# Issuing the first output stores two batches earlier in a batched transposed matmul

## The chip, the cores and the metric

The kernel runs on one core of a Trainium2 chip. The metric is the device time of one execution in microseconds (us). The time before is the median of three runs: 124.31 us, between 124.25 and 124.97. One of these three, the one of 124.97 us, was recorded by the hardware profiler, and every line of a profile below comes from that execution.

## The reference

Sixteen independent products of 512 x 512 matrices in float32, with both operands transposed:

```python
batch, m, k, n = 16, 512, 512, 512
a: (batch, k, m)    b: (batch, n, k)
np.matmul(a.transpose(0, 2, 1), b.transpose(0, 2, 1)).astype(np.float32)
```

Each operand and the output hold 16 matrices of 1 MiB. A core has to read 33.55 MB and to write 16.78 MB.

## The kernel before

The sixteen batches are taken as eight pairs. Each engine has its own program; they meet at semaphores only, and inside one engine the order is the written order.

**Loads (SP).** SP issues all loads, on one DMA queue (q1 in the profile). One load brings both matrices of b of a pair (2 MiB, L122). For the pairs 1 to 5 one load brings both matrices of a (2 MiB, L103); for the pairs 0, 6 and 7 each matrix of a is a load of its own (1 MiB, L105). In the 2 MiB loads each partition reads 16 KB in one piece; in the 1 MiB loads 8 KB. There are three buffers for pairs of a, three for pairs of b and five for pairs of output (`OUTS = 5`). Where a load would bring data into a buffer in use, SP waits first: L101 for the matmuls of three pairs ago, L121 for the transposes of three pairs ago. From batch 10 on SP also waits at L125 until the store of five pairs ago has landed; this wait is put in SP's program ahead of the load of a, so that nothing of the pair can be copied into an output buffer which is still being stored. All later loads stand behind this wait in SP's order. So the load of the pair 5 of a waits for the store of pair 0, the load of batch 12 for the store of pair 1, and the load of batch 14 for the store of pair 2.

**Compute.** ACT casts each matrix of a to bf16 (L165 for the wide loads, in two instructions; L167 for the others). DVE casts b to bf16, half a pair at a time (L190). PE transposes b by matmuls with an identity (L243, the function `turn`), DVE copies the transposed b from PSUM to SBUF (L199), and PE multiplies (L257, the function `half`, 8 matmuls for one half of a batch). For every batch DVE copies the first half of the product from PSUM to the output buffer, and ACT the second (both L177). PE's loop over the pairs is: both halves of the even batch, the first transposes of the next pair, the first half of the odd batch, the second transposes, the second half of the odd batch.

**Stores.** The pairs 0 to 4 are stored by ACT, each by one DMA of 2 MiB on ACT's own queue (q10), issued in ACT's program right behind a copy-out (L225, which calls the function at L87; the profile has the issue at L90). A packet of a store holds 8 KB. The pairs 5, 6 and 7 are stored by SP on q1, behind all loads (L131 for 5 and 6, L135 and L137 for the two halves of 7). ACT's program is, for each batch i: cast batch i + 1, copy out batch i, and then, for some i, one store. Which one, `LAG` says (L223):

```python
j, odd = divmod(i - LAG, 2)
if odd and 0 <= j < H - TAIL:
    store(act, j)
```

With `LAG = 3` the pair j (batches 2j and 2j + 1) is stored behind the copy-out of batch 2j + 4.

**Semaphores.** There are twenty. Some serve two waits: `turned` also counts the last copies-out (as `last_go`), `id_go` also tells that ACT has drained (as `half_go`).

Of the kernel before, what the change touches and what calls it, by code (L numbers as in the profile page):

```python
# [11 lines left out]
def kernel(  # L12
# [29 lines left out]
    LOADS = 3  # L42
    PAIRS = 3
    OUTS = 5
    LAG = 3
    TAIL = 3
    H = B // 2
    STORED = H - (H - OUTS) + 1

    stored = tc.alloc_semaphore("stored")  # L50
# [3 lines left out]
    with tc.tile_critical(sync_engine=nc.gpsimd.engine):  # L54
        sb = lambda name, shape, dt: ctx.enter_context(nc.sbuf_tensor(name, shape, dt))
        ps = lambda name, shape, dt: ctx.enter_context(nc.psum_tensor(name, shape, dt))
        sem = tc.alloc_semaphore
# [10 lines left out]
        o_ps = [ps(f"o_ps{s}", [P, MO // 2, N], f32) for s in range(2)]  # L68


        a_in = [sem(f"a_in{s}") for s in range(2 * LOADS - 1)]
        b_in = [sem(f"b_in{s}") for s in range(PAIRS)]
        o_out = [sem(f"o_out{s}") for s in range(H - OUTS)]


        turned = last_go = sem("turned")
        summed = sem("summed")

        id_go = half_go = sem("id_go")

        bc_go = sem("bc_go")
        bt_go = sem("bt_go")
# [4 lines left out]
        def store(eng, j, part=slice(0, 2)):  # L87


            eng.dma_start(  # L90
                out_v[2 * j + part.start:2 * j + part.stop].rearrange("b p mo n -> p b mo n"),
                o_sb[j % OUTS][:, part],
            ).then_inc(o_out[j] if j + OUTS < H else stored, 16)

        def load_a(sp, i):

            q, g = divmod(i, 2)
            s, use = q % LOADS, q // LOADS
            if use:

                sp.wait_ge(summed, MO * (2 * (q - LOADS) + 1) + 1)  # L101
            if q in WIDE:
                sp.dma_start(a_sb[s][:], a_w[q]).then_inc(a_in[2 * s], 16)  # L103
            else:
                sp.dma_start(a_sb[s][:, g * KO:(g + 1) * KO], a_v[i]).then_inc(a_in[2 * s + g], 16)  # L105
# [7 lines left out]
        def run_sp(sp):  # L113
            for i in range(B):
                if i == 0:
                    load_a(sp, 0)


                for p in ([0] if i == 0 else [(i + 1) // 2] if i % 2 and i + 1 < B else []):
                    if p >= PAIRS:  # L120
                        sp.wait_ge(turned, p - PAIRS + 1)  # L121
                    sp.dma_start(b_sb[p % PAIRS][:], b_v[p]).then_inc(b_in[p % PAIRS], 16)  # L122
                if i % 2 == 0 and i // 2 >= OUTS:

                    sp.wait_ge(o_out[i // 2 - OUTS], 16)  # L125
                if i and not (i % 2 and i // 2 in WIDE):
                    load_a(sp, i)

            for j in range(H - TAIL, H - 1):
                sp.wait_ge(summed, MO * (2 * j + 2) + 3)  # L130
                store(sp, j)  # L131

            sp.wait_ge(summed, MO * (B - 1) + 1)
            sp.wait_ge(half_go, 3)
            store(sp, H - 1, slice(0, 1))  # L135
            sp.wait_ge(last_go, H + 1 + 3)
            store(sp, H - 1, slice(1, 2))  # L137

        def run_pool(pool):
# [30 lines left out]
        def copy_out(eng, i, rm, go):  # L170

            q = rm if isinstance(rm, int) else rm.stop - 1
            eng.wait_ge(summed, MO * i + q + 1)
            copy = eng.copy if eng is nc.scalar else eng.tensor_copy
            h = q // 2
            p = rm - 2 * h if isinstance(rm, int) else slice(None)
            copy(o_sb[i // 2 % OUTS][:, i % 2, rm, :], o_ps[h][:, p, :]).then_inc(go, 1)  # L177
# [40 lines left out]
        def run_act(act):  # L218
            cast_a(act, 0)
            for i in range(B - 1):  # L220
                cast_a(act, i + 1)
                copy_out(act, i, slice(2, 4), oa_go)
                j, odd = divmod(i - LAG, 2)  # L223
                if odd and 0 <= j < H - TAIL:
# [5 lines left out]
        def run_pe(pe):  # L230
# [41 lines left out]
            with pe.Fori(0, H) as _i:  # L272
# [6 lines left out]
                half(1, 1)  # L279

        run_sp(nc.sync)
        run_pool(nc.gpsimd)
        run_dve(nc.vector)
# [35 lines left out]
```

## Time and profile before

| what | value |
|---|---|
| time of the profiled execution | 124.97 us |
| its span, first to last instruction | 122.6 us |
| median of the three runs | 124.31 us |
| bytes read / written | 33.55 MB / 16.78 MB |
| mean DMA rate over the span | 411 GB/s |
| busy share PE / ACT / DVE | 70% / 55% / 46% |
| store issues on ACT's queue (pairs 0 to 4) | 42.34, 52.88, 63.98, 82.19, 96.28 us |
| last three store issues on SP's queue | 108.64, 112.52, 116.81 us |

Busy time counts compute instructions; DMA issues are not in it. "ACTq" and "SPq" mark an instruction of an engine's sequencer, here the issue of a DMA. The time to landing of a DMA is counted from its issue to the semaphore that tells its end; several transfers that wait in one queue have overlapping times. The 16 DMA engines of the core serve both queues, q1 and q10.

### The profile page before, as it was taken

How to read it: one execution, taken by the hardware profiler on the slowest of the kernel's cores; microseconds unless marked ns; L12 is line 12 of the kernel's file. 1: busy time of each engine (PE TensorE's matmuls, PEld its weight loads, DVE VectorE, ACT ScalarE, POOL GpSimd, SP SyncE). 2: the span in 40 equal slices, each digit the busy share in tenths (PEclk: the TensorE clock that was granted, in tenths of full speed). 3: DMA queues.
4: the chain of work that ended last, by engine and by line, in shares of the span. 5: the costliest groups of instructions: out<-in, count | busy, mean ns of one | idle time of the engine just before them, and what ended most of it. 6: DMA issues, size and time to landing. Idle time of an engine off the chain costs nothing. (4 is left out here: it accounts for less than half of the span.)

```text
span 122.6 us, 1085 instructions
## 1 busy us (share of the span) xinstructions
PE 85.2 (70%) x392; PEld 49.6 (40%) x400; DVE 56.2 (46%) x48; ACT 66.8 (55%) x44; POOL 0.7 (1%) x6
## 2 busy tenths in 40 slices
PE   0000949799799899979781992985996389979800
PEld 0000913564464365546331660324642237427500
DVE  0005276476937739574239160087549205270300
ACT  4150015778997997987994029976130590470210
POOL 2000000000000000000000000000000000000000
PEclk9999999999999999999998599589999955999997
DMA  3999999999999999999999999999999999999992
GB/s 64 449 428 428 414 446 428 428 428 428 428 428 428 428 412 409 414 417 436 433 417 441 454 417 414 430 428 452 414 422 428 428 428 425 428 428 428 425 428 118
DMA packets 4928, 50.33 MB, mean 411 GB/s; under 512 B 448, under 2 KB 448, under 8 KB 448
## 3 DMA queue, kind: packets, MB, share of 16 engines
q1 hardware_dynamic: 3568, 39.85, 77.1%
q10 hardware_dynamic: 1360, 10.49, 20.2%
HBM read 33.55 MB, written 16.78 MB: 411 GB/s over the span
## 5 line engine op out<-in xcount | busy, mean ns | idle before, releaser
L257 PE MATMUL o_ps<-bt_sb,a_bf 128*128 128x512 bf16 x248 | 64.1, 407 | 8.3 <-PEq L232 7.3
L257 PEld LDWEIGHTS o_ps<-bt_sb,a_bf 128*128 128x128 bf16 x256 | 29.2, 117 | 38.2 <-issue 16.2
L165 ACT CAST a_bf<-a_sb 64x2048 bf16<-64x2048 f32 x20 | 38.0, 1898 | 9.0 <-DMA a_sb<-in_a_dram 8.7
L243 PE MATMUL bt_ps<-identity,b_bf 128*128 128x128 f32 x144 | 23.6, 317 | 22.6 <-PEq L232 22.6
L177 DVE COPY o_sb<-o_ps 128x1024 f32<-128x1024 f32 x16 | 19.6, 1223 | 32.1 <-PE o_ps L257 32.1
L243 PEld LDWEIGHTS bt_ps<-identity,b_bf 128*128 128x128 f32 x144 | 21.6, 211 | 27.8 <-issue 26.8
L190 DVE CAST b_bf<-b_sb 128x2048 bf16<-128x2048 f32 x16 | 19.4, 1220 | 23.2 <-DMA b_sb<-in_b_dram 23.2
L177 ACT COPY o_sb<-o_ps 128x1024 f32<-128x1024 f32 (+1 forms) x17 | 16.4, 963 | 19.5 <-PE o_ps L257 19.4
L167 ACT CAST a_bf<-a_sb 128x2048 bf16<-128x2048 f32 x6 | 11.4, 1901 | 20.5 <-DMA a_sb<-in_a_dram 20.5
L199 DVE COPY bt_sb<-bt_ps 128x1024 f32<-128x1024 f32 x16 | 19.4, 1215 | 3.2 <-PE bt_ps L243 3.2
L167 ACT ACT_TABLE_LOAD x1 | 1.3, 1283 | 0.9 <-PEq L303 0.9
L144 POOL TENSOR_SCALAR_AFFINE_SELECT identity<-identity 128x128 f32<-128x128 f32 x1 | 0.3, 292 | 0.2 <-POOL identity L142 0.2
L142 POOL MEMSET identity<- 128x128 f32 x1 | 0.2, 204 | 0.7 <-POOLq L54 0.7
L303 POOL MEMSET const-bfloat16-1.0<- 128x1 bf16 x1 | 0.1, 101 | 0.0
L303 POOL MEMSET const-uint8-127<- 128x1 uint8 x1 | 0.1, 101 | 0.0
L303 POOL MEMSET const-float32-0.0<- 128x1 f32 x1 | 0.1, 98 | 0.2 <-issue 0.2
L303 POOL MEMSET const-float32-1.0<- 128x1 f32 x1 | 0.1, 98 | 0.0
## 6 DMA issues: line engine op xcount, KB each, us to landing
b_sb<-in_b_dram SPq DMA_DIRECT2D x8, 2048.0 KB, 20.5
a_sb<-in_a_dram SPq DMA_DIRECT2D x5, 2048.0 KB, 19.9
out_dram<-o_sb ACTq DMA_DIRECT2D x5, 2048.0 KB, 18.6
a_sb<-in_a_dram SPq DMA_DIRECT2D x6, 1024.0 KB, 15.6
out_dram<-o_sb SPq DMA_DIRECT2D x2, 2048.0 KB, 12.7
out_dram<-o_sb SPq DMA_DIRECT2D x2, 1024.0 KB, 5.7
```

Source lines behind the costliest of these rows:

```text
L142: pool.memset(identity[:], 0.0).then_inc(id_go, 1)
L144: pool.affine_select(out=identity[:], in_=identity[:], compare_op=mybir.AluOpType.not_equal, fill=1.0, base=0, pattern=[[-1, P]], channel_ ...
L165: copy = act.copy(to[s * P // 2:(s + 1) * P // 2], x[own, s * KO:(s + 1) * KO, :])
L167: copy = act.copy(to[:], x[:, g * KO:(g + 1) * KO, :])
L177: copy(o_sb[i // 2 % OUTS][:, i % 2, rm, :], o_ps[h][:, p, :]).then_inc(go, 1)
L190: dve.tensor_copy(to, x).then_inc(bc_go, n)
L199: dve.tensor_copy(bt_sb[g][:].rearrange("p j (ni r) -> p j ni r", r=NR), bt_ps[:].rearrange("p j r (g ni) -> p g j ni r", g=2)[:, g],).the ...
L243: last = pe.transpose(bt_ps[:, j, r, :], w[:, r, j, :], identity[:])
L257: last = pe.matmul(o_ps[h][:, q, :], a_r[:, rk, 2 * h + q, :], bt_h[:, rk // 2, rk % 2, :], start=(rk == 0), stop=(rk == KO - 1),)
L303: nc = _bacc.Bacc("TRN2", target_bir_lowering=False, num_devices=1)
```

## The change

Three things are edited.

`LAG` becomes 1, so that the pair j is stored behind the copy-out of batch 2j + 2: behind batch 2 for pair 0, 4 for pair 1, 6, 8 and 10 for the pairs 2, 3 and 4.

Semaphores are no longer shared: `last_go` and `half_go` get semaphores of their own, with constants for their own counts, and `a_in` has one more, which makes three.

`o_out`, which had one semaphore for each of the three stores that a load waits for, becomes one for each of the five output buffers; the waits at L125 are for the same three stores as before. With its two more there are twenty-five semaphores in all.

```diff
-    LAG = 3
+    LAG = 1
...
-        a_in = [sem(f"a_in{s}") for s in range(2 * LOADS - 1)]
+        a_in = [sem(f"a_in{s}") for s in range(2 * LOADS)]
         b_in = [sem(f"b_in{s}") for s in range(PAIRS)]
-        o_out = [sem(f"o_out{s}") for s in range(H - OUTS)]
-        turned = last_go = sem("turned")
+        o_out = [sem(f"o_out{s}") for s in range(OUTS)]
+        turned = sem("turned")
         summed = sem("summed")
-        id_go = half_go = sem("id_go")
+        last_go = sem("last_go")
+        half_go = sem("half_go")
+        id_go = sem("id_go")
...
-            ).then_inc(o_out[j] if j + OUTS < H else stored, 16)
+            ).then_inc(o_out[j % OUTS] if j + OUTS < H else stored, 16)
...
-                    sp.wait_ge(o_out[i // 2 - OUTS], 16)
+                    sp.wait_ge(o_out[i // 2 % OUTS], 16 * (i // 2 // OUTS))
...
-            sp.wait_ge(half_go, 3)
+            sp.wait_ge(half_go, 1)
             store(sp, H - 1, slice(0, 1))
-            sp.wait_ge(last_go, H + 1 + 3)
+            sp.wait_ge(last_go, 3)
             store(sp, H - 1, slice(1, 2))
```

## The prediction

> **What bounds the kernel now.** I read first the page's slices: the busy share of the DMA engines, and what they moved.
>
> ```profile
> PEclk9999999999999999999998599589999955999997
> DMA  3999999999999999999999999999999999999992
> GB/s 64 449 428 428 414 446 428 428 428 428 428 428 428 428 412 409 414 417 436 433 417 441 454 417 414 430 428 452 414 422 428 428 428 425 428 428 428 425 428 118
> ```
>
> From the second slice to the last but one the DMA engines are full, at some 428 GB/s. The bytes are the same after the change, so the sum of the traffic can't get shorter; only its order can change, and with it how much traffic is left when the compute ends. So I look at the end: the last copy-out and the last store's issue in the timeline, and that store's row among the DMA issues.
>
> ```profile
> 116.20 0.58 ACT L177 COPY o_sb<-o_ps 128x512 f32<-128x512 f32 x1 [0.32 <-PE o_ps L257]
> 116.81 0.34 SPq L90 DMA_DIRECT2D out_dram<-o_sb  x1
> out_dram<-o_sb SPq DMA_DIRECT2D x1, 1024.0 KB, 4.7
> ```
>
> The last store lands 4.7 us after its issue, at 121.5, and the span ends 1.1 later. The very first load, 1 MiB into an idle machine, took 4.9. So the last store hardly waits for others: both bounds meet here, and a compute end that comes later moves the end one for one.
>
> What sets the compute end? Going back from it, PE works with small gaps to 98.47. There it had stood still, and so had ACT:
>
> ```profile
> 96.27 1.90 ACT L167 CAST a_bf<-a_sb 128x2048 bf16<-128x2048 f32 x1 [5.37 <-DMA a_sb<-in_a_dram]
> 98.47 3.58 PE L257 MATMUL o_ps<-bt_sb,a_bf 128*128 128x512 bf16 x8 [2.41 <-PEq L232]
> ```
>
> ACT waited 5.37 us for a matrix of a, that of batch 13 (issued at 72.42, its row says 23.8 us to landing: 96.2). PE begins batch 13 when it is cast. So the chain is: batch 13 lands at 96.2, 20.6 us of compute follow up to the last issue at 116.81, then 4.7 and 1.1. The question of the change is when batch 13 lands, and that is set by how many bytes of stores get ahead of it.
>
> **How loads and stores share.** The DMA queues in a window in which both are at work, 46 to 62 us (packets, MB, share):
>
> ```profile
> DMA packets 607, 6.81 MB, mean 425 GB/s; under 512 B 48, under 2 KB 48, under 8 KB 48
> q1 hardware_dynamic: 304, 4.46, 65.1%
> q10 hardware_dynamic: 303, 2.35, 34.7%
> ```
>
> One packet of each in turn. A packet of a wide load is 16 KB and of a store 8 KB, so a store takes a third of the rate while it lasts; against a 1 MiB load (8 KB packets) it takes half. From 35.4 us (chosen below) to 96.2, the landing of batch 13, the two queues moved:
>
> ```profile
> DMA packets 2437, 25.86 MB, mean 425 GB/s; under 512 B 208, under 2 KB 208, under 8 KB 208
> q1 hardware_dynamic: 1365, 17.47, 68.0%
> q10 hardware_dynamic: 1072, 8.39, 32.6%
> ```
>
> 8.39 MB are exactly the stores of pairs 0 to 3.
>
> **Step 1, the issue times.** Now the store of pair 0 is issued just ahead of the copy-out of batch 4:
>
> ```profile
> 32.80 1.01 ACT L177 COPY o_sb<-o_ps 128x1024 f32<-128x1024 f32 x1
> ...
> 42.34 0.42 ACTq L90 DMA_DIRECT2D out_dram<-o_sb  x1
> 43.35 1.01 ACT L177 COPY o_sb<-o_ps 128x1024 f32<-128x1024 f32 x1
> ```
>
> The issue runs 1.0 us ahead of the copy's start, since the sequencer goes on while the cast still runs. The same spot behind batch 2 is 32.80 - 1.0 = 31.8. Its first packets came at 46.0, 3.7 after the issue (window by window: none of q10 at 45 to 46, 15 packets at 46 to 47), so now at 31.8 + 3.7 = **35.4**. Each later store j takes the place in ACT's program that j - 1 had: about 42.3, 52.9, 64 and 82 before delays. Each costs ACT's sequencer 0.38 us beside running casts, as now: nothing on a path; without that cover it would be 5 x 0.38, as it is today. One issue stands in each place as before, except that one place is added (batch 2) and one falls away (batch 12).
>
> **Step 2, is ACT's queue ever empty?** At a third of 425, 2.10 MB take 14.8 to 15.1 us; four stores keep q10 at work from 35.4 to about 80.7 for three, 95.8 for four. The fourth must be issued by 77, the fifth by 92, to follow without a hole. Even with their batches 4 us late (step 3) these issues are at 69 and 86. So q10 has work all the time.
>
> **Step 3, the loads.** The 17.47 MB of q1 hold two 1 MiB loads (batches 12 and 13), 2.10 MB, and 15.37 MB of wide packets. Beside them go 15.37 / 2 + 2.10 = 9.79 MB of stores, in place of 8.39. Together 27.26 MB at 425 GB/s are 64.1 us: batch 13 lands at 35.4 + 64.1 = **99.5, 3.3 us later**. The way there, counted back with 7.4 us for a wide load and 4.9 for a narrow one: b of pair 7 at 94.6 (now 91.0), batch 12 at 87.2 (84.3), b of pair 6 at 82.2 (80.2), a of pair 5 at 74.8 (72.7), b of pair 5 at 67.4 (63.2), a of pair 4 at 60.0 (56.0). All later, the first ones by 4.
>
> **Step 4, SP's gates.** This is what speaks for the change. SP waits today for stores before it may load:
>
> ```profile
> SPq L105 <- DMA out_dram<-o_sb: 20.0, 2, 10.7
> SPq L103 <- DMA out_dram<-o_sb: 15.7, 1, 15.7
> ```
>
> The 15.7 end at 61.06, when store 0 lands; q1 then runs dry, and from 62.5 to 64.5 the trace has 0.87 MB of stores and nothing of loads. With store 0 landing near 52 the load of pair 5 is issued some 9 us sooner and q1 is never empty. But a sooner issue only places it behind 2 wide loads that are now late themselves; the sum of step 3 already has q1 full throughout. The next gates (stores 1 and 2, about 67 and 82) open while 15 us of loads are queued. What q1 wins at 62 to 65 is some two thirds of 2 us; what it loses is a third of 10.6 us, 35.4 to 46.0, and the 84 to 86 us gap in q10, now filled.
>
> **Step 5, the end.** From batch 13's cast on nothing in the program changes: +3.3 to the last issue (120.1) and to the span (125.9). Batches 14 and 15 land near 103.6 and 106.1 (the fifth store's rest, then loads alone); their casts are due by 109 and 110. By 99.5 all but 8.9 MB are moved, some 21 us of traffic, so the DMA engines have holes of some 3 us between 110 and 123. No transfer is late next: compute is.
>
> **Step 6, the semaphores.** No wait is added; each waits for the event it waited for before, so neither a gain nor a new stall is there. Five more may have to be cleared: if the 1.1 us behind the last landing and the 2.4 us outside the span were all due to the twenty, five cost 0.9; the row nearest to it has no semaphore work at all, so I take 0 and keep 0 to 0.9.
>
> The sum against the profiled execution: 124.97 + 3.3 = 128.3. That execution lies 0.66 over the median; on the median it is 124.31 + 3.3 = **127.6**.
>
> **Bounds of the unknown.** The stores ahead of batch 13 are at least today's 8.39 MB (0 us) and at most all five, 10.49 MB: 27.96 / 0.425 = 65.8, +5.0. The clock: after gaps of 2.41 and 3.16 us (98.47, 67.10) PE ran at 0.50 for some 4 to 5 us, after one of 1.91 (84.06) it did not. At 98.47 that costs 3.58 against 1.99 for 8 matmuls and 1.91 against 1.20 for the transposes, 2.3 us. By my schedule PE again stands 2 to 3 us ahead of batch 13, so I keep this stretch; without it the sum is 2.3 lower, with one more 2.3 higher.
>
> The Trainium skill, "TensorE: Matmul & The Clock Gate", section "What's actually happening", lets the clock fall after an idle window of about 3.4 us; the 2.41 us row differs from this, and it decides. By that page batch 13 would run at full clock and the sum would be 125.3. The skill's "DMA: Bandwidth & Descriptors", section "Rules for kernel authors", says to issue a DMA early and wait late; that would have the change cost nothing or gain, about 124. The window of 46 to 62 shows the price it leaves out: an early store takes every second packet from loads that compute waits for.
>
> **Rivals.**
> - *The gates decide, no change.* The two dry stretches of q1 (62.5 to 64.5, and part of 79 to 84) were the real loss; the earlier landings fill them, batch 13 lands by 96.2, and the end stays, since the DMA engines were full anyhow: 124 to 124.6. It decides if q10 moves at most 8.39 MB ahead of batch 13, which needs a hole of 10 us in q10 that step 2 doesn't find.
> - *The clock pays it back.* PE's gap ahead of batch 13 stays under 2 us; 127.6 - 2.3 = 125.3, within 1%.
> - *More than that.* The late loads make one more half-clock stretch behind batch 13, or all five stores get ahead: 129 to 130.
> - *Faster.* Mixed traffic ran at 436 GB/s from 54 to 62 us (3.49 MB in 8 us); if the longer mixing kept that instead of 425, 27.26 MB would take 62.5, batch 13 still 1.7 late. For a gain the compute after it must also lose its half-clock stretch: 124.31 + 1.7 - 2.3 = 123.7, not over 1% even so.
> - *Nothing is moved in fact*, since q10 works in order and was backlogged from 46 to 84: true of stores 1 and 2, but not of store 0, and its 10.6 us shift the rest. This would be 124.3.
>
> **The numbers.** A measurement of this kernel can tell about 1%. Main case (batch 13 late by 2 to 5 us): 0.66. More than that: 0.11. No change by the gates, the clock or for lack of a move: 0.17. Faster by over 1%, for a reason that I don't see: 0.06. The range reaches from no change, 124.0, to 130.0.
>
> **What would show it.** First packets of q10 near 35; the SP wait at L103 for a store much shorter; a of pair 4 landing near 60 and batch 13's cast near 99.5; about 9.8 MB of q10 by then; slices below full DMA share near the end; the last issue near 120. It is wrong if q10 has a hole of many us, if batch 13 no longer ends ACT's longest late wait, or if the last 20 us of compute shrink or grow by a half-clock stretch.

## The result and the profile after

The changed kernel takes 128.34 us (median of four runs, 128.15 to 128.50) where the kernel before takes 124.62 in the four runs beside it: 1.030 times as long, with a 95% interval of 1.026 to 1.034. The forecast was 127.6 on a median before of 124.31, +3.3; measured is +3.7. The profiled execution of the changed kernel took 128.15, with a span of 126.3 us, +3.7 on the 122.6 before. In `kernel.py` of the changed kernel all lines from 75 on have moved up by one, so the store is now L89, the wide load L102, the narrow one L104.

The page's slices of the changed kernel (tenths of busy time, GB/s; a slice is 3.2 us):

```profile
PEclk9999999999999999769999959999999855999996
DMA  3999999999999999999999999999999999909975
GB/s 75 454 431 446 394 441 441 431 426 446 400 337 431 449 418 431 431 426 439 439 413 441 415 423 436 420 426 436 433 436 415 423 428 431 423 31 374 415 332 208
```

The DMA engines are as full as before up to some 110 us. Then there is a slice with 31 GB/s. It is cut finer in the windows of the changed kernel; behind the window stand its length, busy times with instruction counts, the granted clock, the DMA share and GB/s:

```profile
104.00:110.00 6.00, 5.75 (x23) 2.96 (x24) 2.36 (x2) 2.60 (x2) 0.00 (x0) 0.76 1.01 427
110.00:114.00 4.00, 3.92 (x17) 1.74 (x16) 1.73 (x2) 2.81 (x2) 0.00 (x0) 1.00 0.18 74
114.00:121.00 7.00, 5.78 (x32) 3.79 (x32) 1.85 (x2) 1.85 (x3) 0.00 (x0) 1.00 1.01 419
121.00:124.60 3.60, 0.00 (x0) 0.00 (x0) 0.00 (x0) 0.33 (x1) 0.00 (x0) 0.91 0.85 350
```

Soon after 110 all loads and the first six stores are done, the next store is issued only at 113.17, when it has been computed, and until then the DMA engines stand still while PE works. In the kernel before, the same engines moved 426 GB/s from 110 to 114. The traffic itself is unchanged (50.33 MB). It has a hole now because the fifth store of ACT's queue, which in the kernel before is issued at 96.28 and runs behind batch 13, has been moved by 101.

The matmuls of batch 13 and the cast ahead of them, in the timeline of the changed kernel (start, duration, engine, line, operation; the idle time before it in brackets):

```profile
101.99 1.90 ACT L166 CAST a_bf<-a_sb 128x2048 bf16<-128x2048 f32 x1 [6.94 <-DMA a_sb<-in_a_dram]
104.19 3.23 PE L256 MATMUL o_ps<-bt_sb,a_bf 128*128 128x512 bf16 x8 [1.50 <-PEq L231]
107.25 1.11 PE L242 MATMUL bt_ps<-identity,b_bf 128*128 128x128 f32 x8
```

ACT now waits 6.94 us for batch 13, in place of 5.37, and gets it at 102.0 in place of 96.3: 5.7 later. The DMA queues from the first store's packets to that moment, in the changed kernel:

```profile
DMA packets 2778, 28.53 MB, mean 426 GB/s; under 512 B 240, under 2 KB 240, under 8 KB 240
q1 hardware_dynamic: 1418, 18.04, 63.5%
q10 hardware_dynamic: 1360, 10.49, 37.0%
```

All five stores of ACT's queue, 10.49 MB, are ahead of batch 13; before it were four, 8.39 MB. And the end, in the timeline and among the DMA issues of the changed kernel:

```profile
120.75 0.58 ACT L176 COPY o_sb<-o_ps 128x512 f32<-128x512 f32 x1 [0.32 <-PE o_ps L256]
121.36 0.34 SPq L89 DMA_DIRECT2D out_dram<-o_sb  x1
out_dram<-o_sb SPq DMA_DIRECT2D x1, 1024.0 KB, 3.9
```

The last store is issued 4.55 us later than before (121.36 against 116.81) and lands in 3.9 us in place of 4.7: the store in front of it has moved its last bytes by 121.5, 0.1 us after the issue. That leaves 3.7.

SP's waits for stores have shrunk, as step 4 of the prediction expected, from 35.7 us to 12.0; the waits of SP in the changed kernel (total, times, longest):

```profile
SPq L104 <- DMA out_dram<-o_sb: 6.7, 2, 4.4
SPq L102 <- DMA out_dram<-o_sb: 5.3, 1, 5.3
```

That gain is real and buys nothing: the load of pair 5's a is issued at 50.9, ten us sooner than before, and lands at 77.1, four and a half us later.

### The profile page after: what moved, and what is told of

Its sections match the earlier page's. It is cut to its first block, busy times and chain, and to the rows that moved or that the text cites. A ratio compares the mean times of both kernels' runs of the same rounds, so it can differ in the third digit from the quotient of the medians.

```text
span 126.3 us, 1085 instructions
## 1 busy us (share of the span) xinstructions
PE 84.5 (67%) x392; PEld 49.1 (39%) x400; DVE 56.1 (44%) x48; ACT 66.7 (53%) x44; POOL 0.7 (1%) x6
## 2 busy tenths in 40 slices
DMA packets 4928, 50.33 MB, mean 399 GB/s; under 512 B 448, under 2 KB 448, under 8 KB 448
## 3 DMA queue, kind: packets, MB, share of 16 engines
q10 hardware_dynamic: 1360, 10.49, 19.6%
```

## Experiments

The theory to test: **the execution ends at the later of two ends.** One is the end of the traffic, which with full DMA engines gives a span of 122.6. The other is the last store's issue plus 4.9 us (126.3 - 121.36 in the change); the last issue follows the landing of batch 13, and this follows the bytes of ACT's queue that go ahead of it. The rivals: the semaphores cost something; each store moved costs a share of its own, or the first store's early start is the whole price; the loads of the earlier batches, which are all late by 2 to 6 us, set the end.

**Only the semaphores (sems_only).**

```diff
-    LAG = 1
+    LAG = 3
```

> The changed kernel with LAG = 3 again: only the five more semaphores are left of the change. My theory (the order of stores and loads is all): batch 13 lands at 96 to 96.5 us as before, the time is that of before, 124.3 to 125.0. Rival (the semaphores cost part of it): up to 0.9 us more, 125.5.

Measured: 124.39 us, 0.9996 times before (0.9987 to 1.0006). The five semaphores cost nothing that can be measured. The profile of this run shows one thing more. PE's clock did not fall ahead of batch 13 (its first 8 matmuls took 1.99 us, where the profile of before has 3.58), and the compute ended 2.3 us sooner than in the profile of before. The last copy-out and the windows behind it:

```profile
113.92 0.58 ACT L176 COPY o_sb<-o_ps 128x512 f32<-128x512 f32 x1 [0.32 <-PE o_ps L256]
...
116.00:120.00 4.00, 0.00 (x0) 0.00 (x0) 0.00 (x0) 0.00 (x0) 0.00 (x0) 0.79 1.01 428
```

The span is 122.6 all the same: from 116 to 120 the DMA engines run at 428 GB/s with no engine computing. So 122.6 is the end of the traffic, and a sooner compute gains nothing. In the kernel before both ends lie within a us of each other: 116.81 + 4.9 is 121.7.

**Only the stores' places (lag_only).** The kernel before, with its twenty semaphores:

```diff
-    LAG = 3
+    LAG = 1
```

> The kernel before with LAG = 1 and its twenty semaphores. My theory: all five stores of ACT's queue (10.5 MB) are ahead of batch 13, which lands near 102.0; 128.0 to 128.6. Rival (the semaphores cost part of it): 127.4 to 127.7.

Measured: 128.31 us, 1.031 (1.029 to 1.033). Batch 13's cast starts at 101.0, one us sooner than forecast, with 10.36 MB of ACT's queue ahead of it. The profiled execution, with 127.33, is the shortest of the five. The whole difference is `LAG`.

**The first store held back (hold_first).**

```diff
-                j, odd = divmod(i - LAG, 2)
-                if odd and 0 <= j < H - TAIL:
+                for j in {4: (0, 1), 6: (2,), 8: (3,), 10: (4,)}.get(i, ()):
                     store(act, j)
```

> The changed kernel, but the store of pair 0 goes back behind batch 4, where pair 1 is stored right after it; pairs 1 to 4 keep the early places. My theory (what counts is the bytes of ACT's queue ahead of batch 13): q10 starts at 46 again, its backlog of 46 to 84 is as before, only the hole of 83 to 86 is filled; 8.8 to 9.3 MB ahead, batch 13 at 97.2 to 98.1, 125.6 to 126.5. Rival (each store moved costs a share of its own): four fifths of 3.7, 127.6. Rival (the first store's start alone is the price): 124.6.

Measured: 126.23 us, 1.013 (1.009 to 1.016), inside the range of the theory and away from both rivals. On the way there my numbers were short: batch 13's cast starts at 99.2, not 97.2 to 98.1, and 9.68 MB are ahead, not 8.8 to 9.3. The two queues from the start to that cast:

```profile
q1 hardware_dynamic: 2466, 31.61, 75.4%
q10 hardware_dynamic: 1245, 9.68, 23.0%
```

What I had left out: with pairs 1 and 2 already queued behind pair 0, the gate for the load of pair 5 makes q1 quite empty from 62 to 66 (q10 1.72 MB, q1 none), and the stores take all of it.

**Only the first store early (first_only).**

```diff
-                j, odd = divmod(i - LAG, 2)
-                if odd and 0 <= j < H - TAIL:
+                for j in {2: (0,), 6: (1,), 8: (2,), 10: (3,), 12: (4,)}.get(i, ()):
                     store(act, j)
```

> The changed kernel, but only pair 0 is stored early, behind batch 2; pairs 1 to 4 are stored behind the batches 6, 8, 10 and 12 as before. My theory (bytes ahead of batch 13): q10 starts at 35, but is empty from 51 until the next store's packets near 57 to 60, so that 7.9 to 8.6 MB are ahead; batch 13 at 95.5 to 97, 124.0 to 125.5. Rival (the first store's start alone is the price): 128.3. Rival (each store a share of its own): 125.4.

Measured: 124.60 us, 1.002 (1.001 to 1.003). Store 0 is issued nine us sooner than before (33.15 against 42.34), and then ACT's queue runs nearly dry until store 1. From 51 to 58 us the queues of this run moved

```profile
q1 hardware_dynamic: 210, 2.92, 97.4%
q10 hardware_dynamic: 18, 0.07, 2.6%
```

and the loads get back what they lent. At batch 13's cast (96.8) four stores, 8.39 MB, are ahead, as before. So the early start alone is not the price, and it is not a sum of shares either: hold_first (+1.8) and first_only (+0.2) together make 2.0, not 3.9. What these runs have in common is that the price follows how much of the fifth store gets ahead of batch 13: nothing here, 1.3 MB in hold_first.

**One batch sooner (lag2).**

```diff
-    LAG = 1
+    LAG = 2
```

> The changed kernel with LAG = 2: each pair is stored one batch sooner than before, one later than in the change. My theory (bytes of ACT's queue ahead of batch 13, 10.5 MB for the change and 8.4 for before): q10 starts near 42 and has no hole, 9.0 to 9.8 MB ahead, batch 13 at 98.3 to 99.5; 126.0 to 127.3. Rival (only the earliest place is too early): 124.4.

Measured: 124.42 us, 1.000 (0.999 to 1.001). The forecast missed, and the number is the rival's; but the rival's reason, that only the earliest place is too early, doesn't hold, since first_only has a store in that place and costs nothing. In lag2 store 0 is issued at 40.07 (in this profile the first stage ran 1.6 us longer), its first packets come at 43.6, and ACT's queue has no hole, as expected. But only 8.69 MB are ahead at batch 13's cast, which starts at 96.9, not 98.3 or later:

```profile
q1 hardware_dynamic: 2468, 31.62, 77.3%
q10 hardware_dynamic: 1125, 8.69, 21.2%
```

Two things were wrong in my numbers: the queue's start, 42 where it was 43.6, and the stores' bytes, 9.0 to 9.8 MB where they were 8.69. From 43.6 on q1 moved 14.06 MB up to the cast, and the two together at 427 GB/s give 43.6 + (14.06 + 8.69) / 0.427 = 96.9, as measured. So half of the step costs far less than half of the bytes: 0.3 MB of 2.1. One part of it can be read off. The kernel before has a dry stretch of q1 (62.5 to 64.5), in which stores moved 0.87 MB alone; from 62 to 64 lag2 moved 0.44 MB of loads beside 0.39 MB of stores. How much each part adds was not tested. The half us by which batch 13 is late is hidden behind the end of the traffic: the last issue comes at 116.4, and the span is 122.7.

**One batch later (lag4).**

```diff
-    LAG = 1
+    LAG = 4
```

> The changed kernel with LAG = 4: each pair is stored one batch later than before. My theory: SP's load of pair 5 waits for store 0 till some 64 to 68, q1 is empty for 5 to 8 us, but the DMA engines stay full with stores; batch 13 lands before 96, the compute ends sooner, and the end stays at what the traffic allows, 124.0 to 125.2. Rival (later stores give back more of the share, as the step from 1 to 3 did): 121 to 123. Rival (the gates now starve the loads): 126 or more.

Measured: 125.08 us, 1.0075 (1.004 to 1.011); the profiled execution, with 126.28, is the longest. There only 6.57 MB are ahead of batch 13, whose cast starts at 94.1, and the last copy-out ends at 112.5, four us sooner than before. It brings nothing. The ten runs fall into two groups, six of 124.7 to 125.1 and four of 126.2 to 126.3, and the trace is of the second. Its span is 124.4, since the traffic falls behind ahead of 80 us: by then 32.13 MB are moved, before it were 33.06. SP waits for stores (39.9 us in all, against 35.7), from 60 to 66 q1 moves nothing, and the rate falls though the DMA engines count as busy for over nine tenths (windows of this run):

```profile
56.00:60.00 4.00, 3.93 (x24) 2.71 (x25) 1.78 (x3) 3.96 (x3) 0.00 (x0) 1.00 0.93 389
60.00:66.00 6.00, 5.02 (x22) 2.26 (x21) 4.62 (x5) 5.12 (x5) 0.00 (x0) 1.00 0.95 374
...
74.00:80.00 6.00, 2.50 (x6) 0.89 (x7) 0.33 (x1) 5.94 (x4) 0.00 (x0) 0.62 0.96 352
```

So the end of the traffic can be moved too. That the gates do it is how I read these rows; no run here holds the gates alone.

**Another order of the last loads (wide7).** `LAG` stays 1:

```diff
-    WIDE = range(1, 6)
+    WIDE = range(1, 7)
```

> The changed kernel (LAG = 1) with the batches 12 and 13 loaded by one DMA of 2 MiB ahead of b of pair 7 (16 KB packets, and two casts of 1.9 us for each of the two matrices). My theory (the landing of the last of b of pair 7 and batch 13 sets the end): that is now b of pair 7, near 99.4 in place of 102.0, and PE goes on with batch 13 some 2 us sooner: 125.5 to 126.7. Rival (the earlier batches, all late by 4 to 6 us, set the end): 128.0 or more.

Measured: 126.95 us, 1.019 (1.015 to 1.023), between the two. The loads did as forecast: batches 12 and 13 land first, b of pair 7 at 98.9. But PE gains little, because DVE works in its written order. In the timeline of this run:

```profile
98.90 1.23 DVE L189 CAST b_bf<-b_sb 128x2048 bf16<-128x2048 f32 x1 [4.63 <-DMA b_sb<-in_b_dram]
100.04 1.22 DVE L176 COPY o_sb<-o_ps 128x1024 f32<-128x1024 f32 x1
101.17 1.22 DVE L198 COPY bt_sb<-bt_ps 128x1024 f32<-128x1024 f32 x1
...
102.69 1.20 PE L242 MATMUL bt_ps<-identity,b_bf 128*128 128x128 f32 x8 [3.28 <-PEq L231]
```

The copy of the transposed b of pair 6, for which PE waits, stands on DVE behind the cast of pair 7's b, and that waits for its load. PE comes to batch 13 at 103.7 (104.2 in the change). The profiled execution, with 127.92 the longest of the four, also has PE at half clock from 104 to 107 (0.52). This run alone doesn't decide between the theory and the rival of the earlier batches.

**Smaller packets (small_packets).** `LAG` stays 1; the ACT stores go out as two DMAs each, with the counts of the waits raised to match:

```diff
-            eng.dma_start(
-                out_v[...].rearrange("b p mo n -> p b mo n"),
-                o_sb[j % OUTS][:, part],
-            )...
+            for m in ((0, 2), (2, 4)) if j < H - TAIL else ((0, 4),):
+                eng.dma_start(
+                    out_v[..., :, m[0]:m[1]].rearrange("b p mo n -> p b mo n"),
+                    o_sb[j % OUTS][:, part, m[0]:m[1]],
+                )...
```

> The changed kernel (LAG = 1) with each store of the pairs 0 to 4 as two DMAs of half the rows, so that a packet holds 4 KB in place of 8. My theory (one packet of each queue in turn): q10 gets some 21% of the rate beside wide loads in place of 35%; b of pair 5 lands near 63 in place of 69.5. The stores then land late (60, 82) and SP's waits for them hold the loads of batches 12 and 14: 125 to 127. Rival (the queues share by bytes): q10 keeps a third, b of pair 5 lands at 69 to 70, 128.3.

Measured: 126.16 us, 1.014 (1.012 to 1.016). The queues from 40 to 60 us in this run:

```profile
q1 hardware_dynamic: 463, 6.80, 80.0%
q10 hardware_dynamic: 454, 1.77, 21.6%
```

463 packets against 454, and 21% of the bytes: the queues take turns by packets, whatever their size. b of pair 5 lands at 62.6, as forecast, where it is 69.5 in the change. The time then seems to have another reason: the stores land late, SP waits 28.2 us for them at the narrow loads, one slice falls to 328 GB/s, and in this profile (of the longest run, 126.97) the traffic ends later, the last copy-out being done at 116.5 already. That these waits alone cost the time was not tested.

**The fifth store only (last_held, tail4).** Two ways to leave the stores of pairs 0 to 3 early and to get the fifth out of the loads' way. In the first it goes back behind batch 12; in the second SP issues it behind all loads, with `LAG` still 1:

```diff
-                j, odd = divmod(i - LAG, 2)
-                if odd and 0 <= j < H - TAIL:
+                for j in {2: (0,), 4: (1,), 6: (2,), 8: (3,), 12: (4,)}.get(i, ()):
                     store(act, j)
```

> The changed kernel, pairs 0 to 3 stored early (behind the batches 2, 4, 6 and 8), only pair 4 goes back behind batch 12. My theory (the end is the later of two: the traffic's end, which gives a span of 122.6, and the last issue plus 4.9; the last issue follows batch 13, and that the bytes of ACT's queue ahead of it): four stores, 8.4 MB, are ahead, batch 13 at 96.5 to 98, the time 124.3 to 125.3. The loads up to the a of pair 5 are as late as in the change, by 4 to 6 us. Rival (these late loads set the end): 127.5 to 128.5.

```diff
-    TAIL = 3
+    TAIL = 4
```

> The changed kernel with TAIL = 4: pair 4 is stored by SP behind all loads, pairs 0 to 3 by ACT early, behind the batches 2, 4, 6 and 8. My theory: four stores, 8.4 MB, are ahead of batch 13, which lands at 96.5 to 98; behind the loads SP's queue has one store more, so the traffic has no hole; 124.3 to 125.3. Rival (the loads that are late by 4 to 6 us up to pair 5 set the end): 127.5 to 128.5.

Measured: last_held 124.61 us, 1.002 (1.001 to 1.003); tail4 124.40, 1.000 (0.999 to 1.001). The queues of tail4 from the start to batch 13's cast, and two of its earlier loads, issued at 50.71 and 51.08:

```profile
q1 hardware_dynamic: 2492, 31.82, 77.9%
q10 hardware_dynamic: 1088, 8.39, 20.5%
...
a_sb<-in_a_dram SPq DMA_DIRECT2D x1, 2048.0 KB, 25.7
b_sb<-in_b_dram SPq DMA_DIRECT2D x1, 2048.0 KB, 32.7
```

a of pair 5 lands at 76.4 and b of pair 6 at 83.8, some 3.6 us later than in the kernel before and within 0.7 us of the change. Nonetheless the time is that of before. So the late loads of the earlier batches cost nothing here; the rival falls. With 8.39 MB ahead, batch 13 is cast at 96.7, and the traffic has no hole: 424 GB/s from 110 to 114.

Side by side, from the profiled execution of each run (those of lag_only and lag4 lie 1.0 us below and 1.2 above the median):

| run | MB of ACT's queue ahead of batch 13's cast | cast starts | last issue | span | median |
|---|---|---|---|---|---|
| lag4 | 6.57 | 94.1 | 112.5 | 124.4 | 125.08 |
| before | 8.39 | 96.3 | 116.8 | 122.6 | 124.4 to 124.6 |
| sems_only | 8.39 | 96.4 | 114.5 | 122.6 | 124.39 |
| tail4 | 8.39 | 96.7 | 116.4 | 122.7 | 124.40 |
| last_held | 8.39 | 96.8 | 115.0 | 122.7 | 124.61 |
| first_only | 8.39 | 96.8 | 116.4 | 122.5 | 124.60 |
| lag2 | 8.69 | 96.9 | 116.4 | 122.7 | 124.42 |
| hold_first | 9.68 | 99.2 | 119.6 | 124.5 | 126.23 |
| lag_only | 10.36 | 101.0 | 120.6 | 125.4 | 128.31 |
| the change | 10.49 | 102.0 | 121.4 | 126.3 | 128.34 |

In the last three rows the span is the last issue plus 4.8 to 5.0. In the six above them it stays at 122.5 to 122.7, wherever the last issue lies between 114.5 and 116.8. The two lines cross near 117.7. Each MB ahead of batch 13 costs nothing up to there, and some 2.35 us (1 / 0.425) behind it, an estimate; from hold_first to the change the span grows by 1.8 us for 0.81 MB.

No version here beats the kernel before: its compute already ends just within the time that the traffic needs.

## Why the prediction was right

- **What bounds the kernel.** Right, with one correction. "A compute end that comes later moves the end one for one" holds only from a last issue of 117.7 on; the kernel before has 0.9 us to spare. Sooner compute moves nothing (sems_only).
- **Step 1, the issues.** Forecast 31.8 for the first store, measured 31.43; first packets at 35. "Nothing on a path" for the issues themselves is borne out by first_only and tail4.
- **Step 2, no hole in q10.** Right: 10.49 MB without a break from 35 to 101.
- **Step 3, batch 13.** The mechanism is right and its size too small: 102.0, not 99.5, and all five stores ahead, 10.49 MB, not 9.79. The term that was mis-sized is the stores' share, "9.79 MB". Each DMA also has 16 small packets, which the page counts under "under 512 B" (448 for 28 DMAs), and these take turns like any other: in the window of 46 to 62 of the prediction 304 stand against 303 with them, and by the bytes 272 against 287 without. Beside a wide load, 128 + 16 packets of q1, go 144 packets of q10, 136 of 8 KB: 1.11 MB, not 1.05. For the seven wide and two narrow loads' worth this adds some 0.6 MB, an estimate; measured are 0.7. In addition q1 moved 18.04 MB in place of 17.47: 0.3 from the sooner start, and 0.3 since at the cast it has moved 0.5 MB of batch 14 already, where it had 0.2 before (why, no run tells). Together 28.53 MB in place of 27.26 at 426 GB/s are 3.0 us more; the start at 35.0 in place of 35.4 takes 0.4 off. So batch 13 is 5.7 late, outside the main case's "2 to 5 us" and past the bound of +5.0 for all five stores, which left q1's 17.47 MB as they were.
- **Step 4, the gates.** Right: they open sooner, and it gains nothing since q1 is never empty afterwards.
- **Step 5, the end.** "+3.3 from batch 13's cast on" failed in its parts: the delay was 5.7, and 2.0 came back. PE was at half clock for less long (3.23 and 1.11 us for the two steps at 104 in place of 3.58 and 1.91: 1.2 us), which the prediction had priced at up to 2.3 and not expected; and the last store lands 0.8 sooner, because the traffic in front of it is gone. So the total of +3.7 is near the forecast partly by luck: the two errors go against each other. The hole of some 3 us between 110 and 123 is there: 4 us with 74 GB/s.
- **Step 6, the semaphores.** Right: 0.
- **The rivals.** The gates did not decide. The clock paid back half of its price, not enough, though its condition came true: PE stood only 1.50 us ahead of batch 13, but the clock had fallen one step before. The transposes of the change, in its timeline:

```profile
88.21 1.20 PE L242 MATMUL bt_ps<-identity,b_bf 128*128 128x128 f32 x8 [3.20 <-PEq L231]
100.73 1.95 PE L242 MATMUL bt_ps<-identity,b_bf 128*128 128x128 f32 x8 [2.85 <-PEq L231]
```

After a gap of 3.20 us they ran at the full clock, after one of 2.85 at 0.50, so the length of the gap alone, by which the prediction went (2.41 against 1.91), doesn't decide. Its "4 to 5 us" at 0.50 is short for the stretch at 98.47 (0.50 up to 104) and long for the one at 67.10 (0.50 up to 70). "More than that" named all five stores getting ahead, which is what happened at a stated chance of 0.11, though the time, 128.34, lies nearer to the main case's 127.6 than to its 129 to 130. That nothing is moved in fact is refuted by the 35 us start of q10.
- **The pages.** The Trainium skill, "DMA: Bandwidth & Descriptors", section "Rules for kernel authors", would have DMAs issued early; here the early issue costs 3.7 us, and tail4 shows that it is the one store which it puts ahead of the last loads. The same page's section "Queues, rings and completion order" says that each DMA engine takes the queues in turn, and a whole packet of typically 9 to 17 descriptors from one before it switches. The turns are seen here; the packets that the records count are single pieces of 16, 8 or 4 KB beside the small ones, and it is by these that the queues come out even (463 against 454 in small_packets).

## What to carry to other kernels

In a kernel that is limited by its traffic, as this one is, a store that nobody waits for is not free: it takes turns with the loads, and every byte ahead of the last load that compute waits for comes out of the traffic which could run while the last batches are computed. Compare two ends, that of the traffic and that of the last issue plus its landing, and count the bytes ahead of the last awaited load; as long as the first end is the later, an order that delays the other loads costs nothing. What set a queue's share here is the size of its packets, the 16 small ones of each DMA included.

## What was not expected

- Halving the step (lag2) costs nothing, the full step 3.7 us: the price has a threshold, since the traffic's end hides the first us, and with lag2 only 0.3 MB more get ahead of batch 13.
- When the second queue begins, the rate falls for a while: 333 GB/s from 34 to 37 us in the change, 348 from 45 to 47 before. The fall begins up to a us ahead of the second queue's first packets (35.0 and 46.0). Why, no run here tells.
- The first stage took some 1.6 to 1.9 us longer in some profiles (the first store of lag_only is issued at 33.35, of the change at 31.43); the times of the two kernels are the same, 128.31 and 128.34, as one would expect where batch 13's landing is set by the traffic.
